# Steps of a layer norm placed between the tiles of a projection, and some stores issued by another engine

## The chip, the cores and the metric

The kernel runs on one core of a Trainium2 chip. The metric is the device time of one execution in microseconds (us). The kernel before takes 2107.7 us, the median of three runs (2107.07 to 2108.31).

## What is computed

Two transformer blocks run one after the other on 512 tokens of width 1024, in float32. The change lies in the second one. It puts 16 meta tokens ahead, makes a layer norm `h`, and multiplies it with one wide matrix. The columns feed a convolution branch, a recurrence (RWKV-7) and two sets of gates:

```
p = h @ w_in
c = p[..., :1024] * sigmoid(p[..., 1024:2048])          # convolution branch
c = causal_dwconv(c, conv_dw) + conv_dw_b                # 31 taps per channel
y_conv = silu(layer_norm(c, conv_ln_g, conv_ln_b)) @ w_conv_out
y_rwkv = rwkv7_time_mix(p[..., 2048:r_end], ...)         # recurrence, ends in "o @ w_rwkv_out"
gates = sigmoid(p[..., r_end:] + b_gate)
y = gates[..., :1024] * y_conv + gates[..., 1024:] * y_rwkv
h = layer_norm(ALPHA * h + y @ w_o, ln1_g, ln1_b)        # then the feed-forward part
```

## The kernel before

In the second block all activations lie feature by feature: a tile holds 128 features (partitions) by 516 tokens in use, eight tiles make 1024 features, and each is worked on in two halves of 258 tokens (`M2`). To get float32 precision a matrix product is made of three: each operand is split into a high and a low half, the high one by a copy on ScalarE, the low one by a subtraction on VectorE (`halve`, L158), and `mm3` (L191) multiplies high by high, high by low and low by high. One output tile of 128 features is 8 x 3 matmuls for each of two halves, 48 in all (`fm_mm`, L1137). Its weights come by `wcols` (L1134): a load of 512 KB on SP's queue into one of two buffers `wr`, then the split into `wh` and `wl`, two buffers of each.

The order of the work is not written out by hand. Every instruction has a priority, the planner estimates when each is ready, and on each engine it lines up the ready one with the lowest number; `tc.high_priority` shifts the numbers of a block and `at` (L1669) sets them for a stage. The engines then execute their own queue strictly in that order, and wait where an input is late. DMAs are in the queue of the engine that issues them, mostly SP's. Memory comes from pools of a fixed number of buffers for each tag: `P` has 12, `R` has 38, and PSUM's `m2` has 4 banks, which the projections (two for a tile) and the norms share.

Around the change the work is this. Ten gate tiles (`gate_tile`, L1607) are made early, as filler: matmuls, a Tanh on ScalarE into a tile of `P`, and a store to DRAM on SP's queue (L1609). They all start from the same priority. The convolution's eight tiles lie in DRAM too (`CVD`, stored in L1595). `conv_norm` (L1652) loads them back into `P` (`cvl`, L1656) and norms them with `ln_fm` (L1613) in three steps for each half: step 0 sums the eight tiles on VectorE, takes the mean over the partitions by a matmul with a constant matrix (L1628) and subtracts it; step 1 squares on ScalarE, sums on VectorE, takes the variance by a matmul (L1643), then square root and reciprocal; step 2 multiplies. The block runs at the priority of stage `n`, ahead of what follows. Behind it `CS` is made (L1721): Silu on ScalarE and a split of each tile into two of `R`. The recurrence's output `OS` is loaded back and split as well, 14 tiles of `R` (L1715).

Then three projections follow. `mix` (L1729) with `OS` makes the recurrence's output projection, eight tiles; for each, a stored gate is loaded (`sgl`, L1734) and `put` (L1744) takes the two banks out on VectorE, times the gate, into a tile `yr` of pool `P`. This block has a priority of its own, `OFF["r"]`. The second `mix`, with `CS`, does the same for the convolution, and `wo_half` (L1765) multiplies with `w_o`. `ln_fm` is called once more behind it.

Of the kernel before, what the change touches and what calls it, by code (L numbers as in the profile page):

```python
# [12 lines left out]
F32R = mybir.dt.float32r  # L13
I32 = mybir.dt.int32
AF = mybir.ActivationFunctionType
# [76 lines left out]
def tile_blocks(ctx: ExitStack, tc: tile.TileContext, a, out, dbg=None):  # L92
    nc = tc.nc
    V, A, G, TE, SY = nc.vector, nc.scalar, nc.gpsimd, nc.tensor, nc.sync
# [12 lines left out]
    pm = block1.enter_context(tc.tile_pool(name="psumb", bufs=1, space=PSUM, reuse_waits="tile"))  # L107
# [6 lines left out]
    def U(tag, name, dt=F32, n=512):  # L114
        if tag == "H":
            return up.tile([128, 532], dt, name=name, tag=tag, bufs=NU[tag])
        p = {"T": ut, "M": ua, "D": ua, "O": ua, "P": ua}.get(tag, u1)
        return p.tile([128, 512], dt, name=name, tag=tag, bufs=NU[tag])[:, :n]
# [20 lines left out]
    def C(name, rows=128):  # L139
        g, o, w = _COFF[name]  # L140
        return csts[g][:rows, o:o + w]
# [16 lines left out]
    def halve(r, h, l):  # L158

        A.activation(h, r, AF.Copy)  # L160
        V.tensor_tensor(l, r, h, op=OP.subtract)  # L161

    def split_t(dh, dl, src, scale=None):
        if scale is None:
            halve(src, dh, dl)
        else:
            A.activation(dh, src, AF.Copy, scale=scale)
            V.scalar_tensor_tensor(dl, src, scale, dh, op0=OP.mult, op1=OP.subtract)  # L168
# [134 lines left out]
    for i in range(3):  # L303
# [10 lines left out]
        def body(bp, p, i=i):  # L314
            t = U("E", "cn").rearrange("p (s c) -> p s c", s=2)
            evac(t, p)
            CN[i, bp] = t
# [40 lines left out]
    for lst, gv, f, ci, c0 in ((cq, gq, 0, 0, 0), (cq, gq, 1, 0, 128), (cq, gq, 2, 1, 0),  # L358
# [4 lines left out]
        h_, l_ = U("C", "ch", F32R), U("C", "cl", F32R)  # L363
# [344 lines left out]
    pm = block1.enter_context(tc.tile_pool(name="psumc", bufs=1, space=PSUM, reuse_waits="tile"))  # L708
# [219 lines left out]
    with tc.If(nmax > _CAP):  # L928
# [5 lines left out]
        with tc.For_i(0, E_, 1) as ei:  # L934
# [7 lines left out]
            for r in range(4):  # L942
                oh = U("T", "fo").rearrange("p (b j) -> p b j", b=4)
                sh = sm.tile([128, 8], F32, name="sh", bufs=1)
                for b in range(4):
                    for hf in range(2):
# [3 lines left out]
                                        None, op0=OP.is_equal)  # L950
# [29 lines left out]
                for hf in range(2):  # L980
                    py = ps("py")
                    for f in range(2):
                        TE.matmul(py, hT[:, f * 128:(f + 1) * 128], wd[2 * f + hf],
                                  start=(f == 0), stop=(f == 1))
# [111 lines left out]
    TYN = N2 - TY  # L1096
# [10 lines left out]
    def m2ps(n=264):  # L1107
        return [m1ps()[:, :n] for _ in range(2)]

    def m1ps():  # L1110
        return pp.tile([128, 512], F32, name="m2", tag="m2", bufs=4)
# [7 lines left out]
    def hv(p, *ts, n=264, o=0):  # L1119

        return [(p[s],) + tuple(t[:, o + s * n:o + (s + 1) * n] for t in ts) for s in range(2)]
# [12 lines left out]
    def wcols(w, c0):  # L1134
        return wtile([(slice(0, 8), slice(0, 128), kview(w)[:, :, c0:c0 + 128])], 8, 128)

    def fm_mm(o, wh, wl, rh, rl, n=264, o0=0):  # L1137

        for s in range(2):
            cs = slice(o0 + s * n, o0 + (s + 1) * n)  # L1140
            for k in range(8):
                mm3(o[s], wh[:, k], wl[:, k], rh[k][:, cs], rl[k][:, cs], k == 0, k == 7)
# [13 lines left out]
    def P1(name, n=N2, dt=F32):  # L1156
        return u4.tile([128, 532], dt, name=name, tag="P", bufs=12)[:, :n]
# [439 lines left out]
    def gate(f, tile_=TH):  # L1597

        wh, wl = wcols(w2, GC + 128 * f)
        p = m2ps(M2)  # L1600
        fm_mm(p, wh, wl, HH, HL, M2, TY)
        t = tile_("sg")[:, :TYN]
        for q, u in hv(p, t, n=M2):
            A.activation(u, q, AF.Tanh, scale=0.5, bias=bgh[:, f:f + 1])
        return t

    def gate_tile(f):  # L1607
        GT[f] = tc.dram_tile([128, TYN], F32, name=f"gate{f}")
        SY.dma_start(GT[f], gate(f, P1))  # L1609

    onesD = C("onesD")

    def ln_fm(ts, body, order, pre):  # L1613


        hs = [[t[:, s * M2:(s + 1) * M2] for t in ts] for s in range(2)]
        rd = [None] * 2
        for step, s in order:
            if step == 0:
                pm = m1ps()[:, :M2]  # L1620

                acc = P1("lsum", M2)
                V.tensor_tensor(acc, hs[s][0], hs[s][1], op=OP.add)
                for t in hs[s][2:pre]:
                    V.tensor_tensor(acc, acc, t, op=OP.add)
                rows = [acc] + hs[s][pre:]
                for f, t in enumerate(rows):
                    TE.matmul(pm, onesD, t, start=(f == 0), stop=(f == len(rows) - 1))  # L1628
                for t in hs[s]:
                    V.tensor_tensor(t, t, pm, op=OP.subtract)  # L1630
            elif step == 1:
                pv = m1ps()[:, :M2]
                for f, t in enumerate(hs[s]):
                    q = P1("lsq", M2)
                    A.activation(q, t, AF.Square)
                    if pre < 8:
                        TE.matmul(pv, onesD, q, start=(f == 0), stop=(f == 7))
                    elif f == 0:
                        acc = q
                    else:  # L1640
                        V.tensor_tensor(acc, acc, q, op=OP.add)
                if pre == 8:
                    TE.matmul(pv, onesD, acc, start=True, stop=True)  # L1643
                rd[s] = P1("rd", M2)
                A.activation(rd[s], pv, AF.Sqrt, bias=lneps)
                V.reciprocal(rd[s], rd[s])
            else:
                for f, t in enumerate(hs[s]):
                    V.tensor_tensor(t, t, rd[s], op=OP.mult)
                    body(s, f, t)  # L1650

    def conv_norm():  # L1652

        for f in range(8):
            CV.append(P1("cvl", TYN))
            SY.dma_start(CV[f], CVD[f])  # L1656
        ln_fm(CV, lambda s, f, t: None, [(i, s) for i in range(3) for s in range(2)], 8)

    class Z:
        pass  # L1660
# [3 lines left out]
    GT, CV = {}, []  # L1664
# [4 lines left out]
    def at(stage, j):  # L1669
        return tc.high_priority(offset=tc.cur_priority - (B0 + STEP * j + OFF[stage]))  # L1670
    NG = (0, 0, 0, 0, 0, 0, 0, 0, 0, 10)
    gates = [(gate_tile, f) for f in list(range(8, 16)) + list(range(8))]
    fills = [([(conv_tile, s)] if s < 8 else []) + gates[NG[s]:NG[s + 1]] for s in range(9)]

    def fill(s):
        for fn, i in fills[s]:
            with at("c" if fn is conv_tile else "g", s):
                fn(i)
# [3 lines left out]
    def stage(n, fn, j):  # L1682
        with at(n, j):
            fn(j, zs[j])
# [4 lines left out]
    for j in range(8):  # L1689
        if j < 7:  # L1690
            stage("p", stage_p, j + 1)
        fill(j + 1)
        if j < 7:
            stage("x", stage_x, j + 1)
        else:
            with at("n", 0):
                conv_norm()
        stage("y", stage_y, j)
        if j < 7:
            zs[j] = None  # L1700
# [14 lines left out]
    for j in range(7):  # L1715
        r_, l_, h_ = U("R", "osr")[:, :TYN], U("R", "osl", F32R)[:, :TYN], U("R", "osh", F32R)[:, :TYN]
# [2 lines left out]
        OS.append((h_, l_))  # L1719
    OS.append(zs[7].os)  # L1720
    CS = []  # L1721
    for f in range(8):
        t = CV[f]
        A.activation(t, t, AF.Silu, scale=clg[:, f:f + 1], bias=clb[:, f:f + 1])
        h_, l_ = U("R", "csh", F32R)[:, :TYN], U("R", "csl", F32R)[:, :TYN]
        split_t(h_, l_, t)
        CS.append((h_, l_))

    def mix(g0, wout, src, body):  # L1729

        for f in range(8):
            if g0 + f in GT:
                sg = TH("sgl")[:, :TYN]
                SY.dma_start(sg, GT[g0 + f])  # L1734
            else:
                sg = gate(g0 + f)
            wh, wl = wcols(wout, 128 * f)
            p = m2ps(M2)
            fm_mm(p, wh, wl, [t[0] for t in src], [t[1] for t in src], M2, 0)
            body(f, sg, p)  # L1740

    YR = []

    def put(f, sg, p):  # L1744
        t = P1("yr", TYN)
        for q, u, v_ in hv(p, t, sg, n=M2):
            V.scalar_tensor_tensor(u, v_, 1.0, q, op0=OP.add, op1=OP.mult)
        YR.append(t)
    with tc.high_priority(offset=OFF["r"]):
        mix(8, a["w_rwkv_out_2"][0], OS, put)  # L1750
    YS = []

    def put(f, sg, p):
# [4 lines left out]
        split_t(h_, l_, YR[f], 0.5)  # L1758
        YS.append((h_, l_))
    mix(0, a["w_conv_out_2"][0], CS, put)  # L1760

    AL = 2.0 ** 0.25
    H1 = []
# [18 lines left out]
    def body(s, f, t):  # L1782
        V.tensor_scalar(t, t, l1g[:, f:f + 1], l1b[:, f:f + 1], op0=OP.mult, op1=OP.add)
        cs = slice(s * M2, (s + 1) * M2)
        split_t(HH[f][:, cs], HL[f][:, cs], t)
    ln_fm(H1, body, ((0, 0), (1, 0), (0, 1), (1, 1), (2, 0), (2, 1)), 6)

    fdw = sm.tile([128, 44, 3], F32, name="fdw")
    fdv = a["ffn_dw_2"][0].rearrange("j (k p) -> p k j", p=128)
# [4 lines left out]
    for b in range(4):  # L1794
        for s in range(2):
# [6 lines left out]
            t = U("R", "ac")[:, :512]  # L1802
# [40 lines left out]
    for c0, c1 in ((0, 4), (4, 7), (7, 9), (9, 11)):  # L1843
        if c1 == 11:

            WD = {}
            for k in range(2 * (c1 - c0)):
                for q in range(2):
                    r = TH("wdr")[:, :512]
                    SY.dma_start(r, kd[:, 2 * c0 + k, 512 * q:512 * q + 512])  # L1850
                    h_, l_ = P1("wdh", 512, F32R), U("R", "wdl", F32R)[:, :512]
# [3 lines left out]
        for c in range(c0, c1):  # L1855
            for m in range(2):
                f = 2 * c + m
# [4 lines left out]
                h_, l_ = U("R", "zh", F32R)[:, :512], U("R", "zl", F32R)[:, :512]  # L1862
# [54 lines left out]
```

## Time and profile before

| | |
|---|---|
| median of three runs | 2107.7 us |
| the profiled execution, its own time | 2098.6 us |
| its span, first to last instruction | 2096.8 us |
| TensorE busy | 1959.9 us (93%) |
| VectorE busy | 1334.0 us (64%) |
| ScalarE busy | 833.4 us (40%) |
| mean granted clock of TensorE | 0.977 |

The profile is one execution of the program. All times in it count from its first instruction. PE is TensorE, PEld its weight loads, DVE VectorE, ACT ScalarE, SPq the queue of DMAs that SP issues. L1628 is line 1628 of the kernel; where a helper issues the instruction, the line is the helper's, and the tile names tell the work: `osh` and `osl` are the recurrence's output, `csh` and `csl` the convolution's, `hh` and `hl` the normed input, `lsum` and `lsq` the sums of a norm. The time in square brackets behind a timeline's row is the idle time of the engine before it and what ended it. PEclk is the granted clock, 1.00 for 2.4 GHz and 0.50 for 1.2 GHz. A float32 matmul with the constant matrix stands as two records.

### The profile page before, as it was taken

The page shows a single profiled execution, that of the slowest core. Times are in us where ns is not written, and L with a number is a line of the kernel's source. Part 1 is how long each engine was busy: PE and PEld are TensorE (multiplying, and loading weights), DVE is VectorE, ACT ScalarE, POOL GpSimd, SP SyncE. Part 2 cuts the span into 40 slices and gives each one's busy share as a digit, 9 for nine tenths or more (in the row PEclk, how much of TensorE's full clock was granted, in tenths as well). Part 3 has the DMA queues.
Part 4 walks back from the last instruction along what each step waited for, and adds up shares of the span by engine and source line. Part 5 has one row for each costly group of instructions (what it writes and reads, how often), then busy time and mean ns, then how long its engine had stood idle before and what let it go on. Part 6 is the DMA issues. An engine that isn't in the chain of part 4 may idle for free.

```text
span 2096.8 us, 41283 instructions
## 1 busy us (share of the span) xinstructions
PE 1959.9 (93%) x17057; PEld 1656.7 (79%) x17057; DVE 1334.0 (64%) x2957; ACT 833.4 (40%) x1751; POOL 33.9 (2%) x101
## 2 busy tenths in 40 slices
PE   7999999997798999899999999989699989999998
PEld 7778687886454555699888888878599989899997
DVE  4789835443244333779999989995643586455566
ACT  5443544332111100756655656544433253233333
POOL 0000000000000000100000000000000000000000
PEclk9999999998899999899999999999799999999999
DMA  5112021344888997331122111214343323332331
GB/s 160 56 31 82 21 81 41 101 149 154 339 331 338 359 354 262 46 83 50 40 58 66 47 42 57 60 34 121 129 125 91 107 70 93 99 92 91 91 116 50
DMA packets 236963, 247.36 MB, mean 118 GB/s; under 512 B 32156, under 2 KB 190787, under 8 KB 236771
## 3 DMA queue, kind: packets, MB, share of 16 engines
q1 hardware_dynamic: 233315, 234.19, 34.5%
q0 software_dynamic: 2304, 8.39, 1.1%
q8 instruction: 136, 2.23, 0.4%
q10 hardware_dynamic: 1152, 2.10, 0.3%
q14 instruction: 56, 0.46, 0.1%
HBM read 233.79 MB, written 10.84 MB: 117 GB/s over the span
## 4 chain that ended last, share of the span: by engine, by line
PE 68%; DVE 13%; issue 13%; ACT 4%; DMA 1%; POOL 1%; SPq 0%; DVEq 0%; ACTq 0%; POOLq 0%
PE m L194 11%; PE m L192 10%; PE m L193 10%; PE ps L192 5%; PE ps L193 4%; PE ps L194 4%; DVE cv L1593 3%; PE ps L430 2%; DVE wl L161 2%; PE q L192 2%; PE q L194 2%; PE q L193 2%; PE ps L448 1%; PE ps L887 1%; PE y L1532 1%
## 5 line engine op out<-in xcount | busy, mean ns | idle before, releaser
L192 PE MATMUL m<-hh,wh 128*128 128x258 f32 (+1 forms) x1648 | 468.0, 290 | 6.8 <-ACT wh L160 3.0
L194 PE MATMUL m<-hh,wl 128*128 128x258 f32 (+1 forms) x1648 | 466.5, 290 | 2.1 <-DVE wl L161 2.1
L193 PE MATMUL m<-hl,wh 128*128 128x258 f32 (+1 forms) x1648 | 465.8, 288 | 1.8 <-DVE hl L161 1.6
L161 DVE TENSOR_TENSOR wl<-wr,wh 128x1024 fp32r<-128x1024 f32 (+1 forms) x205 | 248.1, 1212 | 228.3 <-ACT wh L160 227.2
L160 ACT ACTIVATE wh<-wr 128x1024 fp32r<-128x1024 f32 (+1 forms) x205 | 214.8, 1050 | 377.9 <-PE m L193 222.6
L192 PEld LDWEIGHTS m<-hh,wh 128*128 128x128 f32 x1648 | 308.6, 190 | 13.1 <-ACT wh L160 3.8
L193 PEld LDWEIGHTS m<-hl,wh 128*128 128x128 f32 x1648 | 309.0, 190 | 6.4 <-DVE hl L161 2.6
L194 PEld LDWEIGHTS m<-hh,wl 128*128 128x128 f32 x1648 | 307.9, 190 | 7.0 <-DVE wl L161 3.4
L1593 DVE SCALAR_TENSOR_TENSOR cv<-th,vec,cv 128x516 f32<-128x516 f32 (+9 forms) x240 | 176.5, 738 | 2.6
L887 PE MATMUL ps<-we,xg 128*64 128x256 f32 x1024 | 130.8, 386 | 5.8 <-PEq L928 5.8
L887 PEld LDWEIGHTS ps<-we,xg 128*64 128x64 f32 x1024 | 74.5, 138 | 51.3 <-issue 17.1
L192 PE MATMUL ps<-wh,hh 128*128 128x256 f32 x352 | 101.4, 288 | 0.9 <-ACT wh L160 0.9
L193 PE MATMUL ps<-wl,hh 128*128 128x256 f32 x352 | 101.0, 287 | 0.7 <-DVE wl L161 0.7
L194 PE MATMUL ps<-wh,hl 128*128 128x256 f32 x352 | 100.8, 287 | 0.0
L192 PEld LDWEIGHTS ps<-wh,hh 128*128 128x128 f32 x352 | 67.1, 191 | 2.0 <-ACT wh L160 1.3
L193 PEld LDWEIGHTS ps<-wl,hh 128*128 128x128 f32 x352 | 67.2, 191 | 1.5 <-DVE wl L161 1.0
L194 PEld LDWEIGHTS ps<-wh,hl 128*128 128x128 f32 x352 | 67.2, 191 | 0.3 <-DVE hl L168 0.2
L902 PE MATMUL ps<-we,hT 128*64 128x512 f32 x256 | 60.7, 615 | 3.8 <-ACT hT L154 3.3
L1031 PE MATMUL ps<-yph,oht 128*128 128x512 f32 x128 | 56.7, 443 | 6.6 <-DVE x L1033 3.6
L890 ACT ACTIVATE hd<-ps,cw 128x256 f32<-128x256 f32 x16 | 7.6, 474 | 135.1 <-PE ps L887 135.1
L1813 ACT ACTIVATE uu<-m 128x258 f32<-128x258 f32 x88 | 33.2, 379 | 65.0 <-PE m L194 65.0
L192 PE MATMUL q<-wh,zh 128*128 128x512 f32 x144 | 56.7, 396 | 0.4 <-DVE ac L1878 0.2
(561 smaller groups left out, 4187.2 us busy)
## 6 DMA issues: line engine op xcount, KB each, us to landing
wr<-in_w_in_dram SPq DMA_DIRECT2D x94, 512.0 KB
we<-in_w_gate_dram SPq DMA_DIRECT2D x64, 512.0 KB
we<-in_w_up_dram SPq DMA_DIRECT2D x64, 512.0 KB
we<-in_w_down_dram SPq DMA_DIRECT2D x64, 512.0 KB
wr<-in_ffn_up_dram SPq DMA_DIRECT2D x44, 512.0 KB
wr<-in_ffn_down_dram SPq DMA_DIRECT2D x18, 512.0 KB
wr<-in_w_out_dram SPq DMA_DIRECT2D x8, 512.0 KB
wr<-in_w_rwkv_out_dram SPq DMA_DIRECT2D x8, 512.0 KB
```

Source lines behind the costliest of these rows:

```text
L160: A.activation(h, r, AF.Copy)
L161: V.tensor_tensor(l, r, h, op=OP.subtract)
L192: TE.matmul(o, lh, rh, start=start, stop=False)
L193: TE.matmul(o, lh, rl, start=False, stop=False)
L194: TE.matmul(o, ll, rh, start=False, stop=stop)
L430: TE.matmul(ss[r], qf(j)[:, bi * 128:(bi + 1) * 128], kf(j)[:, :nk], start=True, stop=True)
L448: TE.matmul(po[r * 64:(r + 1) * 64, f * 128:(f + 1) * 128], v(kb)[:, j * 64:(j + 1) * 64], ptbs[r][:, kb * 128:(kb + 1) * 128], start=(kb ...
L887: TE.matmul(pg[s * 64:(s + 1) * 64, c0:c0 + 256], XG[k][:, s * 64:(s + 1) * 64], w[s][k], start=(k == 0), stop=(k == 7))
L902: TE.matmul(py[s * 64:(s + 1) * 64], hT[:, f * 128 + s * 64:f * 128 + (s + 1) * 64], wd[s][f][:, hf * 512:(hf + 1) * 512], start=(f == 0), ...
L1031: TE.matmul(p, oht[:, bs], yp[hf][0], start=(i == 0), stop=False)
L1593: V.scalar_tensor_tensor(cv[:, lo:], th[:, lo - d:N2 - d], cdw[:, f, 30 - d:31 - d], cv[:, lo:], op0=OP.mult, op1=OP.add)
L1813: A.activation(t, q, AF.Copy)
```

## The change

The stores of the ten gate tiles are issued by ScalarE instead of SP. `conv_norm` is taken apart: its eight loads stay where they were (`conv_back`), and the norm becomes a generator that stops at three places. `put` of the recurrence's projection calls it after tiles 0, 2 and 4. The first call makes step 0 of both halves, the second step 1, the third step 2 and after it Silu and split of the eight tiles. The norm's matmuls go through `tc.keep_in_program_order`, so on TensorE they stand where they are written: behind the matmuls of tile 0 (mean) and of tile 2 (variance), and ahead of the next tile's. The other engines' parts are still lined up by priority, now with numbers of the recurrence's projection. The tiles `yr` come from pool `R` instead of `P`.

```diff
     def gate_tile(f):
-        SY.dma_start(GT[f], gate(f, P1))
+        A.dma_start(GT[f], gate(f, P1))
...
-    def ln_fm(ts, body, order, pre):
+    def ln_fm(ts, body, order, pre, mm=None):
...
+        mm = mm or TE.matmul
         for step, s in order:
+            if step == 3:
+                yield
+                continue
...
-                    TE.matmul(pm, onesD, t, start=(f == 0), stop=(f == len(rows) - 1))
+                    mm(pm, onesD, t, start=(f == 0), stop=(f == len(rows) - 1))
...
-                    TE.matmul(pv, onesD, acc, start=True, stop=True)
+                    mm(pv, onesD, acc, start=True, stop=True)
...
-    def conv_norm():
+    def conv_back():
         for f in range(8):
             CV.append(P1("cvl", TYN))
             SY.dma_start(CV[f], CVD[f])
-        ln_fm(CV, lambda s, f, t: None, [(i, s) for i in range(3) for s in range(2)], 8)
...
-                conv_norm()
+                conv_back()
...
     CS = []
-    for f in range(8):
-        t = CV[f]
-        A.activation(t, t, AF.Silu, scale=clg[:, f:f + 1], bias=clb[:, f:f + 1])
-        h_, l_ = U("R", "csh", F32R)[:, :TYN], U("R", "csl", F32R)[:, :TYN]
-        split_t(h_, l_, t)
-        CS.append((h_, l_))
+    def conv_norm():
+        def mm(*args, **kw):
+            tc.keep_in_program_order(TE.matmul(*args, **kw))
+        yield from ln_fm(CV, lambda s, f, t: None, ((0, 0), (0, 1), (3, 0), (1, 0), (1, 1), (3, 0), (2, 0), (2, 1)), 8, mm)
+        for t in CV:
+            A.activation(t, t, AF.Silu, scale=clg[:, len(CS):len(CS) + 1], bias=clb[:, len(CS):len(CS) + 1])
+            h_, l_ = U("R", "csh", F32R)[:, :TYN], U("R", "csl", F32R)[:, :TYN]
+            split_t(h_, l_, t)
+            CS.append((h_, l_))
+        yield
...
+    norm = conv_norm()
     def put(f, sg, p):
-        t = P1("yr", TYN)
+        t = U("R", "yr")[:, :TYN]
...
         YR.append(t)
+        if f in (0, 2, 4):
+            next(norm)
```

The second call of `ln_fm`, behind the output projection, runs the generator to its end at once and is unchanged in effect.

## Rows read from the trace of the kernel before

**Rows 1.** The page's first part: busy time, share of the span, instructions.
```profile
PE 1959.9 (93%) x17057; PEld 1656.7 (79%) x17057; DVE 1334.0 (64%) x2957; ACT 833.4 (40%) x1751; POOL 33.9 (2%) x101
```
**Rows 2.** Windows: stretch, length, busy time by engine, PEclk, DMA share, GB/s.
```profile
1447.00:1487.10 40.10, 36.14 (x291) 34.88 (x289) 13.05 (x16) 15.09 (x27) 0.00 (x0) 1.00 0.67 202
1487.10:1510.90 23.80, 4.16 (x11) 2.29 (x9) 21.36 (x54) 10.45 (x22) 0.00 (x0) 0.56 0.28 93
1510.90:1558.40 47.50, 47.50 (x386) 47.41 (x385) 24.29 (x39) 19.06 (x25) 0.00 (x0) 0.97 0.42 117
1558.40:1685.40 127.00, 127.00 (x1058) 126.86 (x1057) 58.78 (x90) 33.51 (x42) 0.00 (x0) 1.00 0.33 94
```
**Rows 3.** Timeline of TensorE, gates' end to the projection: start, duration, instruction, [idle before].
```profile
1486.87 0.39 PE L194 MATMUL m<-hh,wl 128*128 128x258 f32 x2
1491.08 2.06 PE L1628 MATMUL m<-lsum,cst 128*128 128x258 f32 x4 [3.82 <-DVE lsum L1625]
1502.27 1.23 PE L1643 MATMUL m<-lsq,cst 128*128 128x258 f32 x2 [9.13 <-DVE lsq L1641]
1510.19 1.23 PE L1643 MATMUL m<-lsq,cst 128*128 128x258 f32 x2 [6.69 <-DVE lsq L1641]
1510.86 0.78 PE L192 MATMUL m<-osh,wh 128*128 128x258 f32 x1
```
**Rows 4.** Timeline of ScalarE: conversions of weights, high half.
```profile
1429.29 1.06 ACT L160 ACTIVATE wh<-wr 128x1024 fp32r<-128x1024 f32 x1
...
1486.95 2.01 ACT L160 ACTIVATE wh<-wr 128x1024 fp32r<-128x1024 f32 x2 [4.43 <-PE m L193]
```
**Rows 5.** The chain of waits from 1480 to 1512, shares by line.
```profile
by line: DMA cvl<-conv 21.0%; DVE lsq L1641 18.1%; DVE cvl L1630 16.1%; DVE lsum L1625 11.2%; issue 10.9%; PE m L1643 7.7%; DVE rd L1646 5.5%; DVE wl L161 3.7%; DVE lsum L1623 2.0%; ACT rd L1645 1.5%; DVE cvl L1649 1.1%; PE m L193 0.7%; PE 
```
**Rows 6.** Waits of TensorE in the gate stage, 1447 to 1487: total, times, longest.
```profile
PE m L192 <- ACT wh L160: 2.4, 3, 0.8
PE m L194 <- DVE wl L161: 1.6, 3, 0.5
```
**Rows 7.** Timeline of VectorE through the norm.
```profile
1491.18 1.22 DVE L161 TENSOR_TENSOR wl<-wr,wh 128x1024 fp32r<-128x1024 f32 x1
1492.32 5.42 DVE L1630 TENSOR_TENSOR cvl<-cvl,m 128x258 f32<-128x258 f32 x16
...
1497.99 1.22 DVE L161 TENSOR_TENSOR wl<-wr,wh 128x1024 fp32r<-128x1024 f32 x1
...
1506.34 0.42 DVE L1641 TENSOR_TENSOR lsq<-lsq 128x258 f32<-128x258 f32 x1
...
1509.72 0.42 DVE L1641 TENSOR_TENSOR lsq<-lsq 128x258 f32<-128x258 f32 x1
```
**Rows 8.** Timeline of TensorE, two matmuls of the projection's first tile.
```profile
1513.98 0.28 PE L193 MATMUL m<-osl,wh 128*128 128x258 f32 x1
1514.10 0.28 PE L194 MATMUL m<-osh,wl 128*128 128x258 f32 x1
```
**Rows 9.** Timeline of TensorE: the later norm's matmuls with the constant matrix.
```profile
1695.53 3.75 PE L1637 MATMUL m<-lsq,cst 128*128 128x258 f32 x16 [1.20 <-ACT lsq L1635]
```
**Rows 10.** Groups by line, 1486 to 1529: count, busy us, mean ns, idle before.
```profile
L161 DVE TENSOR_TENSOR csl<-cvl,csh 128x516 fp32r<-128x516 f32 x8 | 5.5, 692 | 0.6 <-ACT csh L160 0.5
L1646 DVE RECIPROCAL rd<-rd 128x258 f32<-128x258 f32 x2 | 3.5, 1766 | 3.0 <-ACT rd L1645 3.0
...
L1724 ACT ACTIVATE cvl<-cvl,vec 128x516 f32<-128x516 f32 x8 | 6.4, 807 | 1.0 <-DVE cvl L1649 1.0
L160 ACT ACTIVATE csh<-cvl 128x516 fp32r<-128x516 f32 x8 | 4.9, 620 | 0.0
```
**Rows 11.** Issues by tile (ns min/median/max, starts), and a wait of SP.
```profile
L685 ACTq DMA_DIRECT2D rows<-x x8: 325/326/343, 462.5 to 503.6; - x8
...
L1609 SPq DMA_DIRECT2D gate<-sg x10: 320/422/1067, 1430.9 to 1489.8; - x10
...
SPq L1609 <- ACT sg L1604: 27.4, 2, 23.8
```

## What the change should do to the time

> **What bounds the kernel now.** I read the busy table of the page first: TensorE is busy for 93% of the span, the next engine for 64% [rows 1]. So the end is moved only by time in which TensorE stands or runs slowly. The table by stage then says where that is around the change [rows 2]. In the stage of the last gates TensorE is busy for 36.1 of 40.1 us; in the recurrence's projection after the norm, and in the two behind it (convolution, output), it is busy for the whole of 47.5 and 127.0 us. Between them lies a stretch of 23.8 us with 4.2 us of TensorE work at a granted clock of 0.56. That is the convolution's norm.
>
> The timeline of TensorE shows what stands there [rows 3]: the last gate matmul is issued at 1486.87, then come the matmuls of the mean, and one pair for each half's variance, each behind a wait (3.8, 9.1 and 6.7 us, all on VectorE), and only at 1510.86 the first matmul of the recurrence's projection. Nothing in that projection needs the norm: it reads the recurrence's output, and its weights had their high half from 1486.95 on, two tiles in 2.0 us [rows 4]. It stands behind the norm only because TensorE takes its instructions in order and the planner put the norm first. The chain of waits agrees: between 1480 and 1512 it runs through the loads of the convolution tiles (21%), VectorE's sums, subtractions and sums of squares (45% together) and the norm's matmuls (8%), and the projection has hardly a share [rows 5]. So the stretch is on the path that sets the end, nearly whole. From 1510.9 on TensorE is full until 1685.4 [rows 2], so what is won ahead of it should arrive at the end; the later stages keep their order.
>
> **The change, part by part.** The sum is made against the profiled execution, whose own time is 2098.6 us with a span of 2096.8; the median of the runs is 2107.7, 9.1 us above. I take a gain in us to be the same in both.
>
> *The start of the projection.* The first tile can start when its high weights are there, about 1488.1 (1486.95 plus one conversion of some 1.05). It then needs the low weights from VectorE. In the gate stage this costs 0.52 us after the first few matmuls [rows 6], so the earliest effective start is 1488.6. The other bound is the trace's own order: there VectorE makes all 14 additions of the mean first and the low weights at 1491.18, ready at about 1492.3 [rows 7], so 1492.2 with the two products already issued. In the new order the low weights of tile 0 stand ahead of the norm in the program, but which of them the planner puts first on VectorE follows from its own estimate of when the convolution tiles land. I take 1490.0, between the two: gain 1510.9 - 1490.0 = 20.9 us, bounds 18.7 and 22.3.
>
> *The clock.* In the kernel before, the projection starts at half the clock (1.2 GHz), with 13 to 14 intervals of some 0.215 us instead of 0.12 from 1510.86 to 1513.98 [rows 2, 3, 8]. Without the idle stretch the engine stays at 2.4 GHz as in the gate stage (1.00): 13 x 0.095 = 1.2 us.
>
> *The norm's own matmuls.* They move into the projection: two matmuls of the mean and two of the variance, each two records in the trace, so 8 records. Sixteen such records of the later norm take 3.75 us at full clock, 0.234 each [rows 9]. Added: 1.9 us.
>
> *The waits at the pins.* A pinned matmul holds every later matmul on TensorE. A tile of the projection is 48 matmuls of 0.12 us, 5.8 us. Tile 0 ends at 1495.8 and the means follow until 1496.7; the sums ended at about 1491 even in the trace, so there is no wait at the first pin. Then VectorE subtracts: 16 in 5.4 us [rows 7], with one weight conversion (1.2) and one half of an evacuation (0.4) among them, until 1503.6. TensorE does tile 1 meanwhile, until 1502.5. Tile 2 needs two banks, and the banks of the mean come free only with the subtractions of their half: some 0.5 us of wait. Tile 2 ends near 1508.8, and there the second pin wants the sum of squares of both halves. The 14 additions take 0.34 us each back to back and 0.67 where they alternate with others (the second half went from 1506 to 1510 that way) [rows 7], so 4.7 to 9.4 us, with 1.8 us of evacuation and weights between: ready at 1510 to 1515. The wait at the second pin is 1.3 to 6 us; I take 3.5, about the middle. Together 4.0 us, bounds 0 and 6.5.
>
> *The rest of the norm* (reciprocals, scaling, Silu, splits) stands after tile 4 and has no matmul. VectorE: 2 x 1.77 for reciprocals, 8 x 0.69 for splits [rows 10], 16 x 0.34 for the scaling (the subtractions' form [rows 7]), 14.5 us; ScalarE: 8 x 0.81 + 8 x 0.62, 11.4 us [rows 10]. Three tiles, 17.4 us, are left to hide it, and most of it can start after the second pin. Cost: nothing. If that cover is gone, the convolution's projection is late; that is the last rival. As a check on capacity: VectorE was busy for 21.4 us in the gap and 24.3 in the projection [rows 2], 45.7 together, against some 54 us from 1487.1 to the new end of the projection. It fits, at 85%, so waits of VectorE's queue are likely, and a stand of the whole is not. ScalarE has 29.5 in the same time.
>
> *The gate stores.* Ten stores leave SP's queue for ScalarE's. Issued by ScalarE, a store of nearly the same size took 0.33 us (eight in the trace), on SP 0.32 to 1.07 [rows 11]. That is some 3.3 us of ScalarE over 60 us in which it is a third busy; each stands right behind the activation that makes its tile, so no other engine is waited for; queued behind it on ScalarE are the splits of the recurrence's output and the next pair's conversions. Bounded: 0 when it is hidden, 3.3 us lost if each stood before a weight conversion on the path. SP's queue loses two waits on ScalarE, 27.4 us in all [rows 11]. Behind the longest, of 23.8 us, which ended with the first store, stood loads of weights; but the second of the two weight buffers had only been converted from 1429.3 on [rows 4], shortly before that store at 1430.9 [rows 11], so the loads could not have come much earlier. The gate stage's own gaps (three waits of 0.8 for the high and three of 0.52 for the low weights, 4.0 us [rows 6]) come from two tiles that run interleaved and free both weight buffers at once; a store elsewhere does not change that. I take nothing, with 4.0 won and 3.3 lost as ends. The Trainium skill, "DMA: Bandwidth & Descriptors", section "Issuing engines are not separate DMA queues", speaks against this part: transfers started by several engines share the same DMA engines, and a second issuer saves only issue time. By that rule the part is worth nothing too, and the first rival below falls away; the trace shows the waits of SP but no load that was late through them.
>
> *The tile yr* moves to another pool: no instruction more or less. That pool has 38 buffers, and 14 for the recurrence, 8 for yr and 16 for the convolution are exactly 38, so nothing else may be live in it.
>
> **Sum:** 20.9 + 1.2 - 1.9 - 4.0 = 16.2 us. The profiled span becomes about 2080.6, the median 2107.7 - 16.2 = 2091.5. With the bounds: at best 22.3 + 1.2 - 1.9 = 21.6 (2086.1); at worst 18.7 + 1.2 - 1.9 - 6.5 = 11.5 (2096.2), and 3.3 less if the stores are in the way (2099.5).
>
> **The rivals.**
> *The stores free more.* If SP's earlier loads also close the gate stage's gaps, 4.0 us come on top: 2087.5 from the middle, 2082 from the best. Against it: the interleaving above.
> *VectorE's order makes the pins long.* If the low weights of tile 2 are queued behind the whole chain of subtractions and squares, only tile 1 covers it. From the first subtraction to the last variance the chain took 1492.3 to 1510.2, 17.9 us [rows 3, 7]; less 5.8 for one tile, 12.1 us of waiting, and the clock falls again (1.2): 20.9 + 1.2 - 1.9 - 12.1 - 1.2 = 6.9 us, 2100.8; with the reciprocals ahead of the next weights, 3.5 more, 2104. For it: the trace itself has the low weights behind 14 additions though their input was there 3 us earlier. Against it: the second tile's went in between the first and the second sum of squares. The Trainium skill, "TensorE: Matmul & The Clock Gate", in "Architectural detail: the array is 16x 32x32, not 1x 128x128", says ScalarE and VectorE are strict first-in first-out; the trace agrees, with that wait of 3 us.
> *It does not do what it says.* If the planner leaves the projection behind the norm after all, because the weights or the recurrence's tiles come late, the gap stays: within 4 us of 2107.7. Against it: the weights stood ready at 1488.
> *Slower: the convolution's tiles come after the projection.* The pool of 38 is exactly full. If one more buffer is held, the last splits wait for the recurrence's tiles, which come free with the last matmul of the projection. If the whole rest then runs in series, 3.5 + 5.4 + 11.4 = 20.3 us, and TensorE restarts at half clock (1.2), the loss is 21.5 and the result 2107.7 - 16.2 + 21.5 = 2113. It decides when over 16 us of it come behind the last tile. Against it: the pool's other tiles, the loaded halves of the recurrence's output, are split in the gate stage, ahead of the projection.
>
> **How the numbers follow.** Forecast 0.68; the stores free more 0.08; long pins 0.13; no effect 0.05; slower 0.06. The predicted time is the forecast's, 2091.5. The range 2083 to 2102 takes in the forecast with its bounds, most of the first rival and the nearer part of the long pins, and leaves out the rest, under 2 in 10. A change of 0.2%, 4.2 us, is about what a measurement of this kernel can tell from none. Faster: 0.68 + 0.08 + 0.08 of the long pins = 0.84. Same: 0.05 + 0.04 = 0.09. Slower: 0.06 and 0.01 of the long pins, 0.07.
>
> **What would show it.** In the changed profile the first product with the recurrence's tiles should be issued near 1490, with four records of the mean after 48 matmuls and four of the variance after 144; the granted clock should stay at 1.00 through it; waits of TensorE on VectorE should sum to some 4 us, nearly all before the variance; the convolution's projection should begin near 1542 without a wait on its tiles. The gate stage should keep its three pairs of gaps. I am wrong if the recurrence's projection still begins after 1505, if the waits at the pins pass 10 us, or if TensorE stands before the convolution's projection.

## The result, and the profile after

The changed kernel takes 2096.1 us, the median of seven runs, against 2107.1 for the kernel before in the same number of runs: a ratio of 0.9939 with a 95% interval of 0.9919 to 0.9958. That is some 11 to 13 us less. I had forecast 16.2 less and 2091.5; the time lies within the range of 2083 to 2102, 4.6 us on the slow side of the forecast and 5.9 from the slow end.

The spans of the two profiled executions differ by only 2.0 us (2096.8 and 2094.8). The profiled execution of the kernel before was a short one (2098.6 against its median of 2107.1), and the work ahead of the change took longer in the other: the second block's first matmul starts at 866.2 before and at 873.3 after, and the last scan of the recurrence (L1295) at 1361.7 and 1369.8. So I compare stages below and not instants. Windows of the changed kernel (stretch, length, busy us of TensorE, of its weight loads, of VectorE, ScalarE and GpSimd, granted clock, DMA share, GB/s):

```profile
1455.20:1495.20 40.00, 36.05 (x289) 34.85 (x288) 12.35 (x14) 14.85 (x26) 0.00 (x0) 1.00 0.68 202
1495.20:1556.50 61.30, 50.24 (x394) 49.00 (x394) 45.51 (x94) 29.45 (x47) 0.00 (x0) 0.94 0.44 127
1556.50:1683.40 126.90, 126.90 (x1060) 126.71 (x1059) 58.87 (x91) 33.72 (x43) 0.00 (x0) 1.00 0.33 94
```

The first row is the gate stage, with the same length, the same 36 us of work and the same clock as in [rows 2], 8 us later. The second row takes the place of two rows there: the norm's 23.8 us and the projection's 47.5, together 71.3, have become 61.3. The third is the rest as far as the norm behind the output projection, 126.9 us against 127.0. The whole gain, 10.0 us in these profiles, lies in the second row, and nothing is given back behind it. But that row still has 11 us in which TensorE does nothing, and a clock under 1.00.

The timeline of TensorE through it, all rows with a wait and all matmuls of the norm, and the last two rows for the clock:

```profile
1496.09 0.39 PE L192 MATMUL m<-osh,wh 128*128 128x258 f32 x1 [0.80 <-ACT wh L160]
...
1497.44 0.39 PE L194 MATMUL m<-osh,wl 128*128 128x258 f32 x1 [0.60 <-DVE wl L161]
...
1502.78 1.03 PE L1730 MATMUL m<-lsum,cst 128*128 128x258 f32 x4
...
1511.22 0.39 PE L194 MATMUL m<-osh,wl 128*128 128x258 f32 x1 [1.16 <-DVE wl L161]
...
1516.59 0.60 PE L1730 MATMUL m<-lsq,cst 128*128 128x258 f32 x2
1525.69 1.23 PE L1730 MATMUL m<-lsq,cst 128*128 128x258 f32 x2 [8.50 <-DVE lsq L1646]
...
1527.14 0.42 PE L194 MATMUL m<-osh,wl 128*128 128x258 f32 x1
1527.36 0.42 PE L192 MATMUL m<-osh,wh 128*128 128x258 f32 x1
```

Set beside [rows 3], the waits of 3.8, 9.1 and 6.7 us have become none before the mean, none before the first half's variance, and 8.5, more than it was, before the second half's. After that wait the matmuls follow each other every 0.21 us again: TensorE is back at 1.2 GHz, as it was at the start of the projection before.

What it waited for stands in the timelines of ScalarE and VectorE from 1516 on:

```profile
1516.66 1.06 ACT L160 ACTIVATE wh<-wr 128x1024 fp32r<-128x1024 f32 x1 [2.23 <-PE m L193]
1517.74 1.28 ACT L1650 ACT_TABLE_LOAD   x1
1519.03 0.48 ACT L1650 ACTIVATE rd<-m,lneps 128x258 f32<-128x258 f32 x1
1519.41 1.02 ACT L1640 ACTIVATE lsq<-cvl 128x258 f32<-128x258 f32 x3
```
```profile
1517.75 1.23 DVE L161 TENSOR_TENSOR wl<-wr,wh 128x1024 fp32r<-128x1024 f32 x1 [0.54 <-ACT wh L160]
1519.54 1.77 DVE L1651 RECIPROCAL rd<-rd 128x258 f32<-128x258 f32 x1 [0.56 <-ACT rd L1650]
1521.22 0.36 DVE L1646 TENSOR_TENSOR lsq<-lsq 128x258 f32<-128x258 f32 x1
1521.50 0.41 DVE L1654 TENSOR_TENSOR cvl<-cvl,rd 128x258 f32<-128x258 f32 x1
...
1525.21 0.42 DVE L1646 TENSOR_TENSOR lsq<-lsq 128x258 f32<-128x258 f32 x1
```

The second half's squares and sums (`lsq`) are queued behind the first half's table load, root and reciprocal (`rd`), and then alternate with the first half's scaling (`cvl<-cvl,rd`). Root, reciprocal and scaling can only begin when the first half's variance has left TensorE, which issues it at 1516.6. Ahead of the root on ScalarE stand also a conversion of weights, which waited 2.23 us for the matmuls of tile 2, and the table load behind it. So TensorE stands at the second variance matmul for a chain that the matmuls just ahead of it set off. What each link of the chain costs by itself was not tried.

### The profile page after: what moved, and what is told of

It is laid out like the page before. It is cut to its first block, busy times and chain, and to the rows that moved or that the text cites. A ratio compares the mean times of both kernels' runs of the same rounds, so it can differ in the third digit from the quotient of the medians.

```text
span 2094.8 us, 41277 instructions
## 1 busy us (share of the span) xinstructions
PE 1964.4 (94%) x17057; PEld 1659.3 (79%) x17057; DVE 1333.6 (64%) x2957; ACT 833.0 (40%) x1751; POOL 33.9 (2%) x101
## 3 DMA queue, kind: packets, MB, share of 16 engines
q8 instruction: 136, 2.23, 0.5%
## 4 chain that ended last, share of the span: by engine, by line
PE 69%; issue 13%; DVE 11%; ACT 5%; DMA 1%; POOL 1%; SPq 0%; DVEq 0%; ACTq 0%; POOLq 0%
PE m L194 11%; PE m L192 11%; PE m L193 10%; PE ps L192 5%; PE ps L193 5%; PE ps L194 5%; DVE cv L1593 2%; PE ps L430 2%; DVE wl L161 2%; PE q L192 2%; PE q L194 2%; PE q L193 2%; PE ps L448 1%; PE ps L887 1%; PE y L1532 1%
## 5 line engine op out<-in xcount | busy, mean ns | idle before, releaser
L887 PE MATMUL ps<-we,xg 128*64 128x256 f32 x1024 | 135.2, 396 | 6.3 <-PEq L928 6.3
```

The lines of the kernel that those rows point to most:

```text
L887: TE.matmul(pg[s * 64:(s + 1) * 64, c0:c0 + 256], XG[k][:, s * 64:(s + 1) * 64], w[s][k], start=(k == 0), stop=(k == 7))
```

## The experiments

A pin is a place between two tiles at which matmuls of the norm stand: the first behind tile 0 (mean), the second behind tile 2 (variance). Theory A: the wait at the second pin is a matter of order, the chain just read. Theory B, which is how I had priced it: VectorE has too much to do before the pin. A first pair of runs tells them apart. Each ratio below is to the kernel before, run beside it: its median was 2105.8 us beside the first two runs and the two parts of the change, 2106.2 beside the last pair, and 2103.8 beside all others. So times of different groups are compared by their ratios, and the length of a stage by the profiles. The stage here is the time from the first product with the recurrence's tiles to the first with the convolution's, in the changed kernel 60.4 us:

```profile
L192 PE MATMUL m<-osh,wh x128: 277/283/780, 1496.1 to 1556.1; 128*128 128x258 f32 x128
...
L192 PE MATMUL m<-csh,wh x128: 277/282/288, 1556.5 to 1636.4; 128*128 128x258 f32 x128
```

**The sums of both halves first.** Step 1 is cut in two, so that the root and the reciprocal of either half come after the variance matmuls of both:

```diff
-                A.activation(rd[s], pv, AF.Sqrt, bias=lneps)
+                pvs[s] = pv
+            elif step == 4:
+                rd[s] = P1("rd", M2)
+                A.activation(rd[s], pvs[s], AF.Sqrt, bias=lneps)
...
-    ... (3, 0), (1, 0), (1, 1), (3, 0), (2, 0), (2, 1)), 8, mm)
+    ... (3, 0), (1, 0), (1, 1), (4, 0), (4, 1), (3, 0), (2, 0), (2, 1)), 8, mm)
```

> The changed kernel, with step 1 of the norm in two: squares, sums and variance matmuls of both halves first, then square roots and reciprocals. Theory A (order): the 8.5 us that TensorE waits at the second pin arise because the second half's sums are queued on VectorE and ScalarE behind the first half's table load, root and reciprocal. Then the wait should fall to 2 to 4 us, the granted clock should stay at 1.00 there, and the kernel should gain 5 to 8 us on the changed one (about 2089). Theory B (capacity): VectorE simply has too much work before the pin; then the wait stays above 7 us and the time stays within 2 us of the changed kernel's.

Measured: 2092.7 us (2088.1 to 2097.3), ratio to before 0.9933 [0.9918, 0.9948]. The wait fell to 3.6 us, as A says, but neither the full clock nor the 5 to 8 us came with it: the stage takes 59.1 us (1495.4 to 1554.5) against 60.4. Timeline of TensorE in that run, its waits from 1519 on:

```profile
1519.92 0.70 PE L1732 MATMUL m<-lsq,cst 128*128 128x258 f32 x2 [3.58 <-DVE lsq L1646]
...
1540.64 0.39 PE L192 MATMUL m<-osh,wh 128*128 128x258 f32 x1 [1.30 <-ACT wh L160]
...
1541.90 0.57 PE L194 MATMUL m<-osh,wl 128*128 128x258 f32 x1 [0.52 <-DVE wl L161]
```

and its windows, PEclk third from the end, behind each of the two places:

```profile
1520.00:1524.00 4.00, 4.00 (x23) 3.94 (x24) 3.35 (x2) 0.48 (x1) 0.00 (x0) 0.68 0.35 107
...
1541.00:1545.00 4.00, 3.48 (x18) 3.28 (x17) 3.25 (x5) 1.06 (x2) 0.00 (x0) 0.62 0.53 140
```

A new wait took part of the gain: the weight conversions of the later tiles now stand on ScalarE behind the Silus and splits of the convolution's tiles, which come in one run from 1530.2 on. And the clock fell twice instead of once, behind the 3.6 us and behind the pair of 1.3 and 0.5 us.

**The second pin one tile later.** In the changed kernel, `if f in (0, 2, 4)` becomes `if f in (0, 3, 4)`.

> The changed kernel with the variance matmuls one tile later (calls after tiles 0, 3 and 4). Theory B (capacity): 5.8 us more of matmuls cover the sums, the wait at the second pin falls from 8.5 to about 2.7 us, gain 5 to 7 us. Theory A (order): the first half's variance also comes one tile later, and the second half's sums still stand behind its root and reciprocal, so the wait stays at 7 to 9 us and the time within 2 us of the changed kernel's.

Measured: 2096.0 us (2094.7 to 2100.0), ratio 0.9954 [0.9938, 0.9971], the same as the changed kernel within the noise; the stage is 61.7 us long. The wait at the second pin (us in total, times, longest):

```profile
PE m L1730 <- DVE lsq L1646: 8.5, 1, 8.5
```

Not a tenth of the wait went away with 5.8 us more of cover. That is against B and for A: the chain starts at the pin itself, so it moves with it.

**Both together.** Sums first, and calls after tiles 0, 3 and 4.

> Sums of both halves first (as in the run before), and the calls after tiles 0, 3 and 4 instead of 0, 2 and 4. Theory A: without the root between them the second half's sums need only VectorE's time, so one tile more (5.8 us) covers the 3.6 us that were left: no wait at the second pin, the clock stays full there. From the gates' end to the first product with the convolution's tiles 60.2 us become some 55 to 57, if the weights still wait behind the Silus on ScalarE (about 2 us, and the fall of the clock after it); time about 2088. If the wait stays near 3.6 us, it is not VectorE's time but something else that is tied to the pin.

Measured: 2092.7 us (2087.2 to 2094.4), ratio 0.9937 [0.9918, 0.9956]. The stage takes 56.5 us, 3.9 less than in the changed kernel; the ratio does not show it. The wait at the second pin is gone: with the order mended, one tile more does cover VectorE's work. In its place TensorE waits once for a bank of a later tile. All its waits from 1485 to 1560, which takes in the end of the gates, and VectorE where it takes the banks out:

```profile
PE m L192 <- DVE yr L1762: 3.7, 1, 3.7
PE m L194 <- DVE wl L161: 1.6, 3, 0.6
PE m L192 <- ACT wh L160: 1.3, 2, 0.8
```
```profile
1545.59 1.42 DVE L1762 SCALAR_TENSOR_TENSOR yr<-sgl,m 128x258 f32<-128x258 f32 x4
```

VectorE takes four banks out at once, late, because the splits of the convolution's tiles stand in front from 1536.8 on, and four of these wait for ScalarE (some 0.5 us each), where the Silus are still in one run. The reciprocals and the scaling ended at 1535.7, before that. Behind the wait the clock falls (0.50 from 1546.1 to 1550).

**The rest of the norm spread as well.** On top of that, Silu and split in batches of 2, 3 and 3 after tiles 4, 5 and 6, each Silu pinned on ScalarE behind the weights of its tile:

```diff
-        if f in (0, 3, 4):
+        if f in (0, 3, 4, 5, 6):
...
-            A.activation(t, t, AF.Silu, ...)
+            tc.keep_in_program_order(A.activation(t, t, AF.Silu, ...))
...
             CS.append((h_, l_))
+            if len(CS) in (2, 5):
+                yield
```

> As the run with the sums first and calls after tiles 0, 3 and 4, and the Silus of the eight tiles pinned on ScalarE in batches of 2, 3 and 3 behind the weight conversions of tiles 4, 5 and 6. Theory: what the sums first did not bring back was weight conversions queued behind 11 us of Silu and splits; with them in between, TensorE waits only at the start of the projection (1.4 us) and once for a low half (1.2). From the gates' end to the first product with the convolution's tiles some 51 us (61.3 in the changed kernel), the time 9 to 11 us under the changed kernel's, about 2086. Rival: the splits of the last tiles come after the projection, and TensorE waits before the convolution's projection instead; then no more than 5 us better.

Measured: 2085.8 us (2083.1 to 2089.5), ratio 0.9914 [0.9898, 0.9930]. That is 18.0 us less than the kernel before takes beside it, where the changed kernel had 11 to 13. The stage takes 50.6 us, 9.8 less than in the changed kernel. Its two first products, the waits of TensorE from 1485 to 1560 (one of 0.5 us is still in the gates), and the window from the gates' end to the convolution's projection:

```profile
L192 PE MATMUL m<-osh,wh x128: 277/283/468, 1497.5 to 1547.7; 128*128 128x258 f32 x128
...
L192 PE MATMUL m<-csh,wh x128: 277/282/288, 1548.1 to 1628.7; 128*128 128x258 f32 x128
```
```profile
PE m L194 <- DVE wl L161: 1.8, 3, 0.7
PE m L192 <- ACT wh L160: 1.3, 2, 0.8
```
```profile
1496.70:1548.00 51.30, 48.70 (x392) 47.76 (x393) 44.32 (x92) 28.93 (x46) 0.00 (x0) 1.00 0.51 146
```

VectorE does nearly the same work as in the changed kernel (44.3 us against 45.5), in 10 us less: the sum of its work did not bound the stage. No wait is longer than 0.8 us, and the clock stays at 1.00. Batches and pinned Silus were not tried one without the other.

**The norm left out.** Steps 0 to 2 of the convolution's norm are left out; Silu and split stay, pinned behind the weights of tile 4.

```diff
-        yield from ln_fm(CV, lambda s, f, t: None, ((0, 0), (0, 1), (3, 0), (1, 0), ...
+        yield from ln_fm(CV, lambda s, f, t: None, ((3, 0), (3, 0)), 8, mm)
...
-            A.activation(t, t, AF.Silu, ...)
+            tc.keep_in_program_order(A.activation(t, t, AF.Silu, ...))
```

> Leaves out the convolution's norm (steps 0 to 2); Silu and splits stay, pinned behind the weights of tile 4. It shows what the norm still costs in the changed kernel: by the rows 8.5 us of wait, 1.2 for a late low half, 1.1 for the half clock after the wait and 1.9 for its matmuls, 12.7 in all. So from the gates' end to the first product with the convolution's tiles about 48 us against 61.3, and a time 11 to 14 us under the changed kernel's, about 2083. If it is much less, the projection is held by something that is not the norm.

Measured: 2080.2 us (2075.7 to 2083.1), ratio 0.9885 [0.9865, 0.9904]. The stage takes 46.8 us:

```profile
L192 PE MATMUL m<-osh,wh x128: 278/282/387, 1493.1 to 1539.6; 128*128 128x258 f32 x128
...
L192 PE MATMUL m<-csh,wh x128: 277/282/288, 1539.9 to 1619.9; 128*128 128x258 f32 x128
```

So in the changed kernel the norm, with its unpinned Silus, still cost 13.6 us (60.4 - 46.8). In the spread version it costs 3.8: some 2 for its matmuls (1.03 for each of the two groups of four records there), the rest mostly short waits for weights.

**The stores alone, and the norm alone.** The two parts of the change, one at a time. The first is the kernel before with

```diff
-        SY.dma_start(GT[f], gate(f, P1))
+        A.dma_start(GT[f], gate(f, P1))
```

> The kernel before with the ten gate stores issued by ScalarE, nothing else. My sum took nothing for them: within 2 us of before. The rival that they free SP's queue: 4 us faster, with fewer gaps in the gate stage. If they stand in the way on ScalarE: up to 3.3 us slower.

Measured: 2103.8 us (2101.1 to 2110.1), ratio 0.9997 [0.9982, 1.0012]: nothing. Its gate stage keeps its three gaps of each kind. SP's queue finds something else to wait for: the 23.8 us behind the first store's tile [rows 11] are replaced by a wait of the weight loads behind VectorE,

```profile
SPq L1128 <- DVE SI L1536: 23.2, 1, 23.2
```

The second is the changed kernel with the stores back on SP.

> The changed kernel with the gate stores back on SP; the norm between the tiles and the other pool for yr stay. If the gain is the norm's alone, within 2 us of the changed kernel's 2096. If the new place of the norm needs the stores off SP (loads of the convolution's tiles or of the projection's weights stand behind them), 3 us or more slower than the changed kernel, with the mean's matmuls or a weight conversion late.

Measured: 2096.8 us (2095.0 to 2097.3), ratio 0.9950 [0.9935, 0.9965], and a stage of 60.3 us with 8.5 at the second pin. The whole gain is the norm's place, with the other pool for `yr`; no run separates these two.

**The gates one after the other.** My sum left the gate stage's gaps alone because I put them down to two interleaved tiles. In the changed kernel each gate now gets a number of its own:

```diff
     def fill(s):
-        for fn, i in fills[s]:
-            with at("c" if fn is conv_tile else "g", s):
+        for k, (fn, i) in enumerate(fills[s]):
+            n = "c" if fn is conv_tile else "g"
+            with tc.high_priority(offset=tc.cur_priority - (B0 + STEP * s + OFF[n] + (60 * k if n == "g" else 0))):
                 fn(i)
```

> The changed kernel, with a priority of its own for each gate tile instead of one for all ten, so that they run one after the other and not two interleaved. My step said that the gate stage's gaps (three of 0.8 and three of 0.5 us) come from two tiles that free both weight buffers at once. If so the gaps go, and the stage is 3 to 4 us shorter, about 2092. If they come from SP's or ScalarE's queue, they stay, within 2 us of the changed kernel. The new order may also disturb the recurrence's last steps that run beside the gates: then slower.

Measured: 2088.0 us (2087.8 to 2089.8), ratio 0.9927 [0.9912, 0.9942]. From the last scan to the first product with the convolution's tiles it takes 181.8 us (1365.8 to 1547.6) against 186.7 in the changed kernel (1369.8 to 1556.5). Waits of TensorE from 1430 on, first in the changed kernel to 1496 and then with the gates apart to 1500, some 18 us into its projection:

```profile
PE m L192 <- ACT wh L160: 3.0, 4, 0.8
PE m L194 <- DVE wl L161: 1.5, 3, 0.5
PE y L1554 <- DVE Yt L1547: 0.7, 1, 0.7
PE m L192 <- ACT sg L1604: 0.6, 1, 0.6
```
```profile
PE m L1731 <- DVE lsum L1630: 2.2, 1, 2.2
```

The gate stage's waits for weights are gone, so the interleaving made them. What is left up to 1500 is a wait of the mean for the convolution's tiles, which are loaded as late as before while the projection begins earlier, at 1482.6. Behind that, the second pin's 8.5 us and a wait of 1.2 for low weights are unchanged.

**Both, beside the changed kernel.** The spread norm and the gates apart in one kernel, and the changed kernel again on the same chip.

> The spread norm (sums first, calls after tiles 0, 3, 4, 5 and 6, Silus pinned in batches) and the gate tiles with a priority of their own. If the two gains are in different places they add: 10 us from the projection and 5 to 8 from the gate stage, a time of 2078 to 2081, and TensorE's waits from 1430 to the convolution's projection no more than 5 us in all. If the earlier start of the projection only moves the wait to the mean's matmuls (2.2 us in the run with the gates apart, since the convolution's tiles are not loaded earlier), up to 3 us less: 2081 to 2084.

> The changed kernel once more, on the same chip as the run beside it, so that the two can be compared directly: about 2096, and 8.5 us of wait at the second pin again, since the order of every engine is fixed.

Measured: 2080.3 us (2078.6 to 2081.5), ratio to before 0.9874 [0.9857, 0.9891], beside 2093.8 (2091.9 to 2100.5) and 0.9943 [0.9926, 0.9959] for the changed kernel, which has its 8.5 us at the second pin again. The gains add: from the last scan to the first product with the convolution's tiles it takes 172.5 us (1368.7 to 1541.2) against 187.2 in the changed kernel beside it (1373.1 to 1560.3), 14.7 less, where the gates apart had 4.9 and the spread norm 8.5 less (178.2) than the first profile of the changed kernel. From 1430 to the convolution's projection TensorE waits for 3.3 us in all:

```profile
PE m L1733 <- DVE lsum L1630: 2.3, 1, 2.3
PE m L192 <- ACT wh L160: 0.5, 1, 0.5
PE m L194 <- DVE wl L161: 0.5, 1, 0.5
```

This is the fastest version with the whole computation, 13.5 us under the changed kernel beside it.

## Why the prediction was right, and which term was mis-sized

*What bounds it.* Right: the gap on TensorE was on the path, and what was won in it arrived at the end. The stretch behind the projection is 126.9 us long, as before.

*The start of the projection.* It begins 1.4 us behind the gates (0.80 for the high and 0.60 for the low weights), at the best of my bounds and 1.5 better than the value I took. The planner put the low weights of tile 0 behind only two of the additions:

```profile
1495.48 0.77 DVE L1628 TENSOR_TENSOR lsum<-cvl 128x258 f32<-128x258 f32 x2 [9.79 <-DMA cvl<-conv]
1496.16 1.22 DVE L161 TENSOR_TENSOR wl<-wr,wh 128x1024 fp32r<-128x1024 f32 x1
```

*The clock and the matmuls.* The half clock at the start is gone, as said, for 1.2 us. It came back in the same size behind the second pin: from 1526.35 to 1528.9 some 12 matmuls again at 0.21 us, and the variance pair ahead of them. The norm's eight records took about what I had, 1.0 us for the mean and 0.6 for the first half's variance.

*The first pin.* No wait, as said.

*The second pin* is the step that failed. I had priced it as VectorE's time for 14 additions, ready at 1510 to 1515 against a tile that ended at 1508.8, so 1.3 to 6 us, and took 3.5. It cost 8.5, and another 1.2 in clock. I had counted the instructions of step 1 and not read them in their order: root and reciprocal of the first half stand ahead of the sums of the second in the queues of ScalarE and VectorE, the scaling stands between these sums, and root, reciprocal and scaling hang on a matmul that itself stands at the pin. The trace of before showed this chain plainly: [rows 3] has the two variance matmuls 8 us apart with nothing between them, and [rows 7] has the second half's sums from 1506.34 to 1509.72 at twice the interval, alternating with the scaling. I read those rows for a duration only. The two runs with the pin one tile later settle it: 8.5 us stay 8.5 as long as the root is in between, and become none when it is not.

*The start of tile 2.* I had 0.5 us for its banks. TensorE did not wait for these but 1.2 us for its low weights, which stand on VectorE behind the 16 subtractions:

```profile
1503.41 5.42 DVE L1635 TENSOR_TENSOR cvl<-cvl,m 128x258 f32<-128x258 f32 x16
...
1509.95 1.22 DVE L161 TENSOR_TENSOR wl<-wr,wh 128x1024 fp32r<-128x1024 f32 x1
```

Together: 5.0 us more at the pin, 0.7 at the weights, 1.2 of clock, less 1.5 at the start, is 5.4 of the 6.2 us by which the stages' gain (10.0) falls short of 16.2. Under 1 us is not accounted for. That the time lies within the range is in part luck. The waits of 8.5 and 1.2 us are outside the 0 to 6.5 that I had given them, and the 10.0 us are less than the 11.5 of my worst sum with hidden stores. A start at the best of its bounds gave some of it back, and the range went on to 2102 for the stores and the long pins, not for this chain.

*The rest of the norm.* Hidden, as said: the convolution's projection starts at 1556.5 without a wait. (I had 1542; 8 us of the difference lie ahead of the gates' end, see above.) It was hidden less freely than I thought; once the pins were shorter, the same Silus held up weights.

*The stores* are worth nothing, as said (0.9997). The Trainium skill, "DMA: Bandwidth & Descriptors", section "Issuing engines are not separate DMA queues", has it that a second issuing engine saves only issue time; the runs agree with it. And the 4.0 us of the gate stage did come from the interleaving. I was wrong to stop at that: a change of priorities takes these gaps away, and more.

*The rivals.* The long pins (2100.8) were the nearest of them in price, but by another mechanism than I gave: not the weights queued behind the norm, which took 1.2 us. The full pool of 38 buffers held nothing up: no wait of TensorE stands before the convolution's projection.

*The pin itself* was given a meaning it did not have here. Without it, with plain matmuls at the same places, the planner writes the same order for every engine, instruction by instruction. What moved the norm was its place in the program, with the priority of the projection.

## What to carry to other kernels

Before work is put between the tiles of a stage, write down its chain across the engines, not its sum on each: a wait at a pinned instruction can be as long as the chain that leads to it from the last thing on the same engine, however much work covers the stretch ahead. When two halves go through such a place, let both reach it before either goes on. And when a wait is removed, look at once at what else was queued in the time that it gave.

## What the runs showed of the hardware

Two things I had not expected. TensorE's clock can fall behind waits that are all short: in the run with the sums first it stood at 1.00 from 1530 to 1540, and waits of 1.30 and 0.52 us (issue resumed at 1540.64 and 1541.90) were followed by matmuls at 1.2 GHz (0.62 of full speed over 1541 to 1545). In the changed kernel a pair of 0.80 and 0.60 at the start of the projection and a single 1.16 in tile 2 left it at 2.4:

```profile
1497.00:1502.00 5.00, 4.56 (x38) 4.57 (x39) 5.00 (x14) 0.72 (x2) 0.00 (x0) 1.00 0.74 227
1511.00:1516.00 5.00, 4.78 (x40) 4.78 (x41) 4.36 (x10) 1.69 (x4) 0.00 (x0) 1.00 0.88 243
```

One profile shows the fall; whether it took both waits is open. And the stages repeat better than the whole: the changed kernel and its version with the stores on SP take 60.3 to 60.7 us between the two first products in three profiles, while the second block's first matmul, behind work that the change leaves alone, starts anywhere from 866.2 to 876.5 in the profiles of this case. A difference of a few microseconds is better read from the stage than from the span.
